# Low parts of weight units: a negated copy and an accumulating DMA in place of a subtraction

## The chip, the cores and the metric

The kernel runs on one core of one Trainium2 chip. Its time is that of one execution on the device, in microseconds; lower is better. A core has five engines that work side by side and wait for each other through semaphores: TensorE (matmuls), VectorE, ScalarE, GpSimd and SyncE, which here only starts transfers. Transfers between the chip's main memory and the core's on-chip memory are run by DMA engines; whichever engine starts one has it in its own queue and goes on.

## The reference

Two layers over 512 tokens of 1024 features, all in float32. Layer 0 mixes the tokens with a Mamba-2 state space (SSD), layer 1 with HGRN2. Behind the mixer of each layer comes a norm, a squared-ReLU MLP with 4096 hidden features, a second norm, and a gate with embeddings `p`:

```python
for i in range(DEPTH):
    mix = ssd_mixer(x, ...) if i % 2 == 0 else hgrn2_mixer(x, ...)
    h = layer_norm(DEEPNORM_ALPHA * x + mix, ln_g[i, 0], ln_b[i, 0])
    h = layer_norm(DEEPNORM_ALPHA * h + sq_relu_mlp(h, mlp_w1[i], mlp_w2[i]), ln_g[i, 1], ln_b[i, 1])
    x = h + jax.nn.sigmoid(h @ ple_w_gate[i]) * (p[i] @ ple_w_proj[i])
```

Nearly all of the arithmetic is matrix products with weights: the mixers' projections in and out (`u @ w_in`, `y @ w_out`), the MLP's `h @ w1` and `(a * a) @ w2`, and the gate's two.

## The kernel before

**Units.** A weight matrix comes in units of 128 partitions by 1024 float32 values, 512 KB. A matrix product in float32 is made as three products in the faster type float32r: both factors are split into a high part (the value rounded to float32r) and a low part (what is left of it), and `mm3` (line 109) makes high x high, high x low and low x high. So each unit needs, before TensorE can use it, a high and a low part. `unit` (line 98) does that for 192 plain units: SyncE loads the unit into a `raw` buffer (line 102), ScalarE casts it into `whi` (line 104), and VectorE subtracts `whi` from `raw` into `wlo` (line 106). `weight_sums` (line 284) does it for another 52 units of the MLP, two at a time, with sums of blocks for Strassen's product; its own casts and subtractions stand at lines 293 and 295.

**Buffers.** There are 3 `raw` buffers (`RAWS`), 5 of `whi` and 5 of `wlo`, used in turn by `unit` and `weight_sums` alike. A load waits until the `raw` buffer's earlier unit has been read by the cast and the subtraction; a cast waits until TensorE has done its last matmul with the earlier unit in that `whi`; TensorE waits for the cast before the first matmul with a high part, and for the subtraction before the first with a low part.

**Stages.** The SSD layer comes first (some 370 us): projections of 24 matmuls a unit (`project`, line 127), between them the scan's steps of each pair of heads, and the output projection. Then the MLP of layer 0: each eighth of the hidden features is projected (`hidden`, line 349), the first three pairs of tiles with plain units and the others with Strassen's products (`strassen`, line 309), and each eighth is projected out (`out_project`, line 225) with four plain units. The order is that of line 32: hidden eighth 0, then 1, then output 0, hidden 2, output 1 and so on; output 7 comes last and the second norm's chunks are made behind each of its four chunks of 128 tokens. An output projection adds, for each half of the columns and each of the four token chunks, twelve matmuls into one PSUM bank: six with the half's first unit, six with its second (`out_part`, line 208). The gate (lines 394 to 430) has, for each half of the columns, one unit of `wp` and four of `wg`, all five held over the four token chunks: six matmuls with the one into `pp`, twenty-four with the others into `pg`. Layer 1 has HGRN in the place of SSD, with the same MLP and gate behind it.

**What sets the order.** The kernel is written on a framework that plans the order of each engine's instructions ahead of time, by priorities and by its own estimates of how long each instruction takes; an engine then executes its own in that order, and waits at the head of it. What stands in `tc.high_priority(offset=LEAD)` (line 100) is planned earlier than its place in the code. Only in HGRN is the order of TensorE's instructions that of the code (`manual_schedule`, line 904), where the projections of later heads fill the waits of a head's scores. TensorE has four PSUM banks for projections (`psj`), so at most four chunks can be open at once.

The kernel's start is written with two units ahead of the others (lines 139 to 150): `first.append(unit(..., 0))`.

Of the kernel before, what the change touches and what calls it, by code (L numbers as in the profile page):

```python
# [27 lines left out]
RAWS = 3  # L28
FIRST = 1000
# the first pairs of hidden tiles are plain products, the others Strassen's  # L30
PLAIN = 3
ORDER = [(w[0], int(w[1])) for w in "h0 b0 h1 o0 h2 o1 h3 o2 h4 o3 h5 o4 h6 o5 h7 o6 o7".split()]
# HGRN: the projections in their order, and how much of them goes between the steps of two heads
# [9 lines left out]
def trunk(ctx: ExitStack, tc, a):  # L43
# [31 lines left out]
    def begin(name):  # L75
        """the pool of temporaries of a phase, in place of the phase before's"""
        if phase:
            phase[1].__exit__(None, None, None)
            phase.clear()
        phase.append(tc.tile_pool(name=name, bufs=1, reuse_waits="tile"))  # L80
        phase.append(phase[0].__enter__())
        phase.reverse()
        phase.append(bufs[name])
# [13 lines left out]
    # ---------------------------------------------------------------- weights  # L97
    def unit(src, lead=LEAD):
        n = src.shape[1]
        with tc.high_priority(offset=lead):  # L100
            raw = mk(raws, [P, 1024], "raw")
            nc.sync.dma_start(raw[:, :n], src)
            hi = mk(whip, [P, 1024], "whi", F32R)
            nc.scalar.copy(hi[:, :n], raw[:, :n])  # L104
            lo = mk(wlop, [P, 1024], "wlo", F32R)
            nc.vector.tensor_sub(lo[:, :n], raw[:, :n], f32(hi[:, :n]))  # L106
        return hi, lo
# [6 lines left out]
    class Split:  # L114
        """[128, n, 512] as high and low parts, in slots of four rows each."""
# [11 lines left out]
    def project(src, xs, ps, m=P, tok=slice(0, T)):  # L127
        """ps[m, tok] = W[:, tile].T @ x.T for a weight unit of eight row tiles."""
        hi, lo = src
        for k in range(8):  # L130
            c = slice(k * m, (k + 1) * m)
            mm3(ps[:m, tok], hi[:, c], lo[:, c], xs.h(k, tok), xs.l(k, tok), k == 0, k == 7)

    # ---------------------------------------------------------------- constants
# [5 lines left out]
    with tc.high_priority(offset=FIRST):  # L140
        for k0, n in ((0, 1), (1, 1), (2, 2), (4, 2), (6, 2)):
            nc.sync.dma_start(xraw[:, k0 : k0 + n, :], a["xT"][:, k0 : k0 + n, :])
            if k0 == 0:
                dtw = mk(raws, [P, 1024], "raw")
                nc.sync.dma_start(dtw[:, :256], a["wdt"])
            elif k0 in (1, 6):
                first.append(unit(a["wssd"][k0 // 4], 0))
            for k in range(k0, k0 + n):
                nc.scalar.copy(x_s.h(k), xraw[:, k, :])
                nc.vector.tensor_sub(x_s.l(k), xraw[:, k, :], f32(x_s.h(k)))  # L150
# [19 lines left out]
    # ---------------------------------------------------------------- layer norm and friends  # L170
# [7 lines left out]
    def layer_norm(c, gb):  # L178
        """acc[:, c] = LN(acc[:, c])"""
        src = acc[:, c, :]  # L180
        st = mk(sm, [P, 2, 6], "lnst")
        for h in range(2):
            nc.vector.bn_stats(st[:, h, :], src[:, h * 512 : (h + 1) * 512])
        mv = mk(sm, [P, 2], "lnmv")
        nc.vector.bn_aggr(mv, st.rearrange("p a b -> p (a b)"))
        sd = mk(sm, [P, 1], "lnsd")
        nc.scalar.activation(sd, mv[:, 1:2], AF.Sqrt, bias=eps)
        rs = mk(sm, [P, 1], "lnrs")
        nc.vector.reciprocal(rs, sd)
        nc.vector.scalar_tensor_tensor(src, src, mv[:, 0:1], gb[0], ALU.subtract, ALU.mult)  # L190
        nc.vector.scalar_tensor_tensor(src, src, rs, gb[1], ALU.mult, ALU.add)

    def transpose_split(src, dst, c, keep=None):
        """dst[:, k, chunk c] = src[tokens, k-th 128 features].T, split; unsplit in keep"""
        sl = slice(c * P, (c + 1) * P)
        for q in range(2):
            pt = bank(pst, "pt")
            for j in range(4):
                k = 4 * q + j
                nc.tensor.transpose(pt[:, j * P : (j + 1) * P], src[:, k * P : (k + 1) * P], ident)  # L200
            v = pt.rearrange("p (j t) -> p j t", j=4)
            h = dst.hi[q][:, :, sl]
            nc.scalar.copy(h, v)
            nc.vector.tensor_sub(dst.lo[q][:, :, sl], v, f32(h))
            if keep is not None:
                nc.scalar.copy(keep[q][:, :, sl], v)

    def out_part(units, n, xs, c, h, first, scale):
        """acc[:, c, half h] += x[:, chunk c].T @ W over n row tiles, each token's row by scale if given;
        acc holds alpha * residual (or the residual, if first)"""  # L210
        sl = slice(c * P, (c + 1) * P)
        ps = bank(psj, "pj")
        for k in range(n):
            hi, lo = units[k // 2]
            ks = slice((k % 2) * 512, (k % 2 + 1) * 512)
            mm3(ps, xs.h(k, sl), xs.l(k, sl), hi[:, ks], lo[:, ks], k == 0, k == n - 1)
        d = acc[:, c, h * 512 : (h + 1) * 512]
        if scale is not None:
            nc.vector.scalar_tensor_tensor(d, ps, scale[:, c : c + 1], d, ALU.mult, ALU.add)
        elif first:  # L220
            nc.vector.scalar_tensor_tensor(d, d, ALPHA, ps, ALU.mult, ALU.add)
        else:
            nc.vector.tensor_add(d, ps, d)  # L223

    def out_project(w, xs, first, after=None, scale=None):
        """w: the four units of four row tiles, by halves of the columns; after(c): what follows the last of chunk c"""
# [12 lines left out]
    def norm(i):  # L239
        """the norm's result, transposed and split, and what makes its chunk c"""  # L240
        gb = ln_params(i)
        h_s = Split(8)
        keep = [mk(b8, [P, 4, T], "b8") for _ in range(2)] if i % 2 == 0 else None

        def chunk(c):
            layer_norm(c, gb)
            transpose_split(acc[:, c, :], h_s, c, keep)

        return h_s, chunk, keep

    # Winograd's form of Strassen's product: seven products of blocks for eight. The blocks of h.T are
    # [token half][k half], those of the weights [k half][output tile].
    def block_sums(h_s, ht):
        """the four plain and four summed blocks of h.T, as (high, low) of a row tile k"""
# [28 lines left out]
    def weight_sums(src1, src2):  # L283
        """the seven blocks of two weight units: B11, B21, B22, T1, T2, T3, B21 - T2, as (high, low, column)"""
# [24 lines left out]
    def strassen(blocks, src1, src2, z):  # L309
        """z[:, m] = W[:, tile m].T @ h.T for two weight units"""  # L310
# [34 lines left out]
    def mlp_and_gate(layer, h_s, ht, last):  # L345
        """acc holds the normed h. Returns the next x, transposed and split, with x in acc."""
# [40 lines left out]
        # gate  # L387
# [45 lines left out]
    # ---------------------------------------------------------------- layer 0: SSD  # L433
    # time steps
# [36 lines left out]
    # dt * exp(cs_last - cs)  # L471
# [6 lines left out]
    def dt_tail():  # L478
        # token-major copies: [128 tokens, chunk, head]
# [10 lines left out]
    def conv_silu(ps, i, out):  # L490
        """out = silu(causal conv of ps + bias), channel tile i of the convolved ones"""
# [50 lines left out]
    def core(j, xs, sz, y, toks, btok, cbm, cm):  # L542
# [3 lines left out]
        # token-major x * dt and x * dt * decay to the chunk's end  # L546
# [11 lines left out]
        # chunk states and their scan  # L558
# [13 lines left out]
        # masked decays times C B  # L572
# [9 lines left out]
        # decay from the chunk's start, on channels  # L582
# [33 lines left out]
    def rms_group(ss):  # L616
        """1 / rms of each token of the group: [128 tokens, chunk]"""
# [52 lines left out]
    # ---------------------------------------------------------------- layer 1: HGRN2  # L670
# [6 lines left out]
    # lower bounds: softmax over the one layer, cumulated, less its first row  # L677
# [11 lines left out]
    # The tensor engine's order is fixed here: the projections of the heads to come fill the waits of a head's scores.  # L689
    def vg(i):  # L690
        """values and output gates of heads 2i and 2i + 1, by tokens: [128, chunk, 256]"""
# [80 lines left out]
    def hcore(h, s, i, hl):  # L772
# [12 lines left out]
        def column_sums(f, n):  # L785
            """the sums over the partitions, on each of them"""
# [8 lines left out]
        # the scores of a token with itself and of an odd one with the token before it  # L795
# [63 lines left out]
        # states  # L859
# [23 lines left out]
        # norm and output gate  # L883
# [57 lines left out]
def _tiles_m(w):  # L941
    """[K, M] -> [M/128, 128, K/128 * 128]: one unit per 128 output channels"""
# [4 lines left out]
def _tiles_g(w):  # L947
    """[K, 1024] -> [K/128, 128, 1024]: per four row tiles, two units for each half of the columns"""
# [5 lines left out]
def _tiles_h(w):  # L954
    """[K, 1024] -> [2 * K/256, 128, 2 * 512]: by halves of the columns, two row tiles each"""
# [5 lines left out]
def _tiles_q(w):  # L961
    """[1024, 1024] -> [4, 2, 128, 4 * 256]: by quarters of the columns, four row tiles each"""
# [4 lines left out]
def _cols(v):  # L967
    """[n * 128] -> [128, n]"""
# [3 lines left out]
def _rows(v):  # L972
    """[K, T] -> [128, K/128, T]"""
# [70 lines left out]
```

## Time and profile before

| | |
|---|---|
| median of 3 runs | 1495.58 us (1493.39 to 1496.82) |
| the profiled execution: span from the first to the last instruction | 1492.3 us |
| TensorE busy | 1479.3 us (99%) |
| VectorE busy | 1096.4 us (73%) |
| ScalarE busy | 711.2 us (48%) |
| GpSimd busy | 0.9 us |
| DMA engines, mean busy share by the loads' queue | 30.1%, 148.67 MB |
| granted TensorE clock | 0.999 |

The page has no time of the profiled execution other than its span; the median of the runs is 3.3 us above it.

How to read the rows: PE is TensorE's matmuls, PEld its loads of stationary operands, DVE VectorE, ACT ScalarE, POOL GpSimd, SPq the queue that SyncE starts transfers from. `wlo<-raw,whi` names what an instruction writes and reads, without buffer numbers; `x192` counts instructions; behind the bar stand the busy time in us, the mean of one in ns, and the idle time of the engine ahead of them with what ended most of it. In a timeline a row begins with its start and its duration in us, and `[0.53 <-DVE wlo L106]` says that the engine was idle for 0.53 us until VectorE's line 106 released it. The durations of matmuls overlap: they follow each other faster than one lasts. L-numbers are lines of the kernel before.

### The profile page before, as it was taken

The page shows a single profiled execution, that of the slowest core. Times are in us where ns is not written, and L with a number is a line of the kernel's source. Part 1 is how long each engine was busy: PE and PEld are TensorE (multiplying, and loading weights), DVE is VectorE, ACT ScalarE, POOL GpSimd, SP SyncE. Part 2 cuts the span into 40 slices and gives each one's busy share as a digit, 9 for nine tenths or more (in the row PEclk, how much of TensorE's full clock was granted, in tenths as well). Part 3 has the DMA queues.
Part 4 walks back from the last instruction along what each step waited for, and adds up shares of the span by engine and source line. Part 5 has one row for each costly group of instructions (what it writes and reads, how often), then busy time and mean ns, then how long its engine had stood idle before and what let it go on. Part 6 is the DMA issues. An engine that isn't in the chain of part 4 may idle for free.

```text
span 1492.3 us, 21964 instructions
## 1 busy us (share of the span) xinstructions
PE 1479.3 (99%) x8848; PEld 1280.9 (86%) x8848; DVE 1096.4 (73%) x1786; ACT 711.2 (48%) x968; POOL 0.9 (0%) x8
## 2 busy tenths in 40 slices
PE   8999999999999999999999999999999999999998
PEld 5888888888989999888778998989898999998887
DVE  6998677797886777776844767769787777777673
ACT  5777455563564434444334453543364444444342
POOL 0000000000000000000000000000000000000000
PEclk9999999999999999999999999999999999999999
DMA  6433223332233323244223222222123333324322
GB/s 237 169 102 111 98 100 113 100 113 85 71 99 99 113 82 103 88 139 129 94 71 114 86 66 77 70 72 72 57 72 99 114 113 100 110 79 150 115 71 71
DMA packets 41621, 150.07 MB, mean 101 GB/s; under 512 B 4624, under 2 KB 5136, under 8 KB 41392
## 3 DMA queue, kind: packets, MB, share of 16 engines
q1 hardware_dynamic: 41520, 148.67, 30.1%
q8 instruction: 70, 1.15, 0.3%
q14 instruction: 31, 0.25, 0.1%
HBM read 146.49 MB, written 2.16 MB: 100 GB/s over the span
## 4 chain that ended last, share of the span: by engine, by line
PE 97%; DMA 1%; DVE 1%; ACT 1%; issue 0%; SPq 0%; ACTq 0%; DVEq 0%
PE pj L110 29%; PE pj L111 28%; PE pj L112 28%; PE py L782 1%; PE py L591 1%; PE pt L200 1%; PE pm L561 1%; PE py L596 1%; PE py L792 1%; PE py L827 1%; DMA raw<-in_wg 1%; DVE wlo L106 0%; PE pt L549 0%; PE py L880 0%; PE py L112 0%; PE py L110 0%
## 5 line engine op out<-in xcount | busy, mean ns | idle before, releaser
L110 PE MATMUL pj<-whi,b 128*128 128x512 f32 (+1 forms) x1096 | 401.5, 367 | 0.5 <-ACT z L414 0.5
L111 PE MATMUL pj<-wlo,b 128*128 128x512 f32 (+1 forms) x1096 | 399.3, 364 | 0.5 <-DVE wlo L106 0.5
L112 PE MATMUL pj<-whi,b 128*128 128x512 f32 (+1 forms) x1096 | 399.8, 365 | 0.0
L110 PE MATMUL pj<-b,whi 128*128 128x256 f32 (+1 forms) x1024 | 348.0, 340 | 2.1 <-ACT whi L104 2.1
L112 PE MATMUL pj<-b,wlo 128*128 128x256 f32 (+1 forms) x1024 | 344.2, 336 | 0.0
L111 PE MATMUL pj<-b,whi 128*128 128x256 f32 (+1 forms) x1024 | 343.7, 336 | 0.0
L104 ACT CAST whi<-raw 128x1024 fp32r<-128x1024 f32 x192 | 201.4, 1050 | 229.6 <-PE pj L111 133.4
L106 DVE TENSOR_TENSOR wlo<-raw,whi 128x1024 fp32r<-128x1024 f32 x192 | 233.9, 1220 | 64.4 <-ACT whi L104 62.4
L111 PEld LDWEIGHTS pj<-wlo,b 128*128 128x128 f32 x1096 | 206.8, 189 | 32.2 <-DVE wlo L106 1.0
L110 PEld LDWEIGHTS pj<-whi,b 128*128 128x128 f32 x1096 | 206.6, 189 | 32.3 <-ACT z L414 0.7
L112 PEld LDWEIGHTS pj<-whi,b 128*128 128x128 f32 x1096 | 206.7, 189 | 31.7 <-issue 0.2
L110 PEld LDWEIGHTS pj<-b,whi 128*128 128x128 f32 x1024 | 194.5, 190 | 22.0 <-ACT whi L104 4.7
L112 PEld LDWEIGHTS pj<-b,wlo 128*128 128x128 f32 x1024 | 194.4, 190 | 20.3 <-DVE b L150 1.7
L111 PEld LDWEIGHTS pj<-b,whi 128*128 128x128 f32 x1024 | 194.6, 190 | 18.3 <-issue 1.9
L293 ACT CAST whi<-raw 128x1024 fp32r<-128x1024 f32 (+1 forms) x52 | 43.4, 835 | 136.2 <-PE pj L112 110.4
L223 DVE TENSOR_TENSOR acc<-pj,acc 128x512 f32<-128x512 f32 x120 | 81.6, 686 | 35.0 <-PE pj L112 34.5
L110 PE MATMUL pj<-S,whi 128*128 128x256 f32 x312 | 87.4, 280 | 0.0
L111 PE MATMUL pj<-S,whi 128*128 128x256 f32 x312 | 87.0, 279 | 0.0
L112 PE MATMUL pj<-S,wlo 128*128 128x256 f32 x312 | 87.0, 279 | 0.0
L295 DVE TENSOR_TENSOR wlo<-raw,whi 128x1024 fp32r<-128x1024 f32 (+1 forms) x52 | 49.7, 957 | 35.0 <-ACT whi L293 35.0
L293 ACT CAST whi<-a 128x1024 fp32r<-128x1024 f32 x26 | 27.3, 1050 | 94.8 <-PE pj L111 45.5
L110 PEld LDWEIGHTS pj<-S,whi 128*128 128x128 f32 x312 | 58.7, 188 | 0.0
(217 smaller groups left out, 1810.6 us busy)
## 6 DMA issues: line engine op xcount, KB each, us to landing
raw<-in_w SPq DMA_DIRECT2D x128, 512.0 KB, 3.4
raw<-in_wssd SPq DMA_DIRECT2D x40, 512.0 KB, 3.4
a<-csd SPq DMA_DIRECT2D x16, 512.0 KB, 4.0
raw<-in_wso SPq DMA_DIRECT2D x16, 512.0 KB, 3.3
raw<-in_wg SPq DMA_DIRECT2D x16, 512.0 KB, 3.8
raw<-in_whvg SPq DMA_DIRECT2D x16, 512.0 KB, 3.3
raw<-in_whq SPq DMA_DIRECT2D x16, 512.0 KB, 3.3
raw<-in_who SPq DMA_DIRECT2D x8, 512.0 KB, 3.3
```

The source lines that it names most:

```text
L104: nc.scalar.copy(hi[:, :n], raw[:, :n])
L106: nc.vector.tensor_sub(lo[:, :n], raw[:, :n], f32(hi[:, :n]))
L110: nc.tensor.matmul(out, sh, mh, start=start, stop=False)
L111: nc.tensor.matmul(out, sh, ml, start=False, stop=False)
L112: nc.tensor.matmul(out, sl, mh, start=False, stop=stop)
L200: nc.tensor.transpose(pt[:, j * P : (j + 1) * P], src[:, k * P : (k + 1) * P], ident)
L223: nc.vector.tensor_add(d, ps, d)
L293: nc.scalar.copy(hi[:, :n], f)
L295: nc.vector.tensor_sub(lo[:, :n], f, f32(hi[:, :n]))
L561: nc.tensor.matmul(pst_[:, c * P : (c + 1) * P], btok[:, c, :], xw[:, c].rearrange("p h q -> p (h q)"), start=True, stop=True)
L591: nc.tensor.matmul(yd[64 * r : 64 * r + 64, sl], xdt[:, 2 * c + r, :], m[:, r, sl], start=True, stop=True)
L596: nc.tensor.matmul(yo[:, c * P : (c + 1) * P], pv[:, c - 1].rearrange("p h q -> p (h q)"), cm[:, c * P : (c + 1) * P], start=True, stop=True,)
```

## The change

In `unit`, all but the first two units (`early=True`) get their low part in another way. ScalarE, having cast `raw` into `whi`, also writes the negative of `whi` into `wlo`. Then a transfer started from GpSimd's queue reads `raw` and adds it to what stands in `wlo`, so that `wlo` holds `raw - whi`. The `raw` buffer is read by that transfer in place of the subtraction, and there are four of them in place of three. The units that `weight_sums` makes for Strassen's products are as before. (The diff also empties the lines of comments; that is left out here.)

```diff
-RAWS = 3
+RAWS = 4
...
-    def unit(src, lead=LEAD):
+    def unit(src, lead=LEAD, early=False):
         n = src.shape[1]
         with tc.high_priority(offset=lead):
             raw = mk(raws, [P, 1024], "raw")
             nc.sync.dma_start(raw[:, :n], src)
             hi = mk(whip, [P, 1024], "whi", F32R)
             nc.scalar.copy(hi[:, :n], raw[:, :n])
             lo = mk(wlop, [P, 1024], "wlo", F32R)
-            nc.vector.tensor_sub(lo[:, :n], raw[:, :n], f32(hi[:, :n]))
+            if early:
+                nc.vector.tensor_sub(lo[:, :n], raw[:, :n], f32(hi[:, :n]))
+            else:
+                nc.scalar.mul(lo[:, :n], f32(hi[:, :n]), -1.0)
+                nc.gpsimd.dma_start(lo[:, :n], raw[:, :n], accum_op=ALU.add)
         return hi, lo
...
-                first.append(unit(a["wssd"][k0 // 4], 0))
+                first.append(unit(a["wssd"][k0 // 4], 0, True))
```

## The prediction

> **What bounds the kernel now.** I read the page first (busy time, groups, DMA issues), then the windows by stage, then who waits for the line that goes, then the timeline at the few places where a weight unit is made just in time.
>
> From the page (engine: busy us, share, instructions; a group's busy us and mean ns; an issue's KB and median us to landing):
>
> ```profile
> span 1492.3 us, 21964 instructions
> PE 1479.3 (99%) x8848; PEld 1280.9 (86%) x8848; DVE 1096.4 (73%) x1786; ACT 711.2 (48%) x968; POOL 0.9 (0%) x8
> ...
> q1 hardware_dynamic: 41520, 148.67, 30.1%
> ...
> L104 ACT CAST whi<-raw 128x1024 fp32r<-128x1024 f32 x192 | 201.4, 1050 | 229.6 <-PE pj L111 133.4
> L106 DVE TENSOR_TENSOR wlo<-raw,whi 128x1024 fp32r<-128x1024 f32 x192 | 233.9, 1220 | 64.4 <-ACT whi L104 62.4
> ...
> raw<-in_w SPq DMA_DIRECT2D x128, 512.0 KB, 3.4
> ...
> a<-csd SPq DMA_DIRECT2D x16, 512.0 KB, 4.0
> ```
>
> TensorE is idle for 1492.3 - 1479.3 = 13.0 us of the span, so nothing that only relieves VectorE can win more. The windows (PE busy of each stretch in its second figure) say where these 13.0 us lie:
>
> ```profile
> 0.00:25.00 25.00, 18.74 (x62) 9.46 (x63) 13.28 (x20) 12.50 (x19) 0.88 (x8) 1.00 0.73 263
> ...
> 415.00:710.00 295.00, 295.00 (x1821) 266.53 (x1820) 213.48 (x300) 130.94 (x142) 0.00 (x0) 1.00 0.34 109
> 710.00:795.00 85.00, 84.22 (x407) 68.16 (x406) 57.20 (x76) 33.09 (x45) 0.00 (x0) 1.00 0.26 86
> 795.00:1065.00 270.00, 268.61 (x1879) 239.17 (x1877) 187.41 (x389) 123.37 (x248) 0.00 (x0) 1.00 0.23 75
> ...
> 1405.00:1492.30 87.30, 82.76 (x401) 68.71 (x399) 52.13 (x71) 26.79 (x36) 0.00 (x0) 0.99 0.22 73
> ```
>
> 6.3 us are the start, 4.5 us the last stretch with its tail, 0.8 and 1.4 us the first gate and HGRN. And of line 106, who waited for it in the whole run:
>
> ```profile
> L106 DVE TENSOR_TENSOR wlo<-raw,whi x192: 1197/1220/1253, 9.2 to 1463.4; 128x1024 fp32r<-128x1024 f32 x192
> ...
>   PEld pj L111: 1.0, 1
>   PE pj L111: 0.5, 1
>   PEld pj L112: 0.4, 1
> ```
>
> TensorE lost 1.9 us to the subtraction that the change removes. That is what there is to win; what there is to lose is decided by how long the replacement takes between "high part made" and "low part there", against the time that TensorE leaves.
>
> **The change part by part.**
>
> *Removed:* 190 of the 192 subtractions, 190 x 1.220 = 232 us of VectorE, 73% to 58%. VectorE isn't the bound and nearly nobody waits for it: worth 0 to 1.9 us.
>
> *Added on ScalarE:* 190 negated copies of 128x1024. The nearest row is an ACTIVATE of that shape (timeline: start us, us):
>
> ```profile
> 508.43 1.06 ACT L370 ACTIVATE z<-z 128x1024 f32<-128x1024 f32 x1
> ```
>
> 190 x 1.06 = 201 us, 48% to 61%. In sum it lies beside the matmuls; where casts follow each other closely it makes each unit take 2.1 us of ScalarE instead of 1.05, which counts below.
>
> *Added on GpSimd's queue and the DMA engines:* 190 transfers of 512 KB that read raw, read lo and write lo. GpSimd is idle (0.9 us busy), and its queue holds nothing else after the start, so waiting there holds up nobody. In bytes, 190 x 0.524 = 99.6 MB; read twice it is 199 MB against the 148.67 MB that take 30.1%, so 40% more: 70% in the mean. Not the bound, but loads and these transfers will meet.
>
> *The time D from issue to landing* of such a transfer isn't in this trace. Below: a load of the same 512 KB, 3.4 us. Above: the largest transfer there is,
>
> ```profile
> acc<-in_x SPq DMA_DIRECT2D x1, 2048.0 KB, 8.7
> ```
>
> 8.7 us for four times the bytes. From the two rows (8.7 - 3.4) / 3 = 1.8 us for each 512 KB and 1.6 us fixed; two streams instead of one give 1.6 + 2 x 1.8 = 5.2 us. I take 5.4 us, with 0.2 us for landing beside the loads (the csd row, landing among them, is 4.0 and not 3.4), and keep 3.4 and 8.7 for the range. The Trainium skill, DMA: Bandwidth & Descriptors, section Anatomy of one DMA — SWDGE (gpsimd) path, gives a fixed 2.0 us plus bytes / 436e3, an estimate of 3.2 us here for one pass; no run here shows a transfer from that queue.
>
> *Moved, the wait.* The low part is now ready D + 1.06 us after the cast ends, before it was 1.2 us. So at every unit I compare that with the time from the cast's end to TensorE's first use of the low part. Where the casts run several units ahead of TensorE, in the SSD stage and most of HGRN, I cost it at nothing; that lead hides it. The lead is gone where the five slots of whi and wlo are all in use and a cast waits for TensorE to free one. ScalarE's and TensorE's rows there:
>
> ```profile
> 507.48 1.05 ACT L104 CAST whi<-raw 128x1024 fp32r<-128x1024 f32 x1 [0.82 <-PE pj L111]
> ...
> 513.16 1.05 ACT L104 CAST whi<-raw 128x1024 fp32r<-128x1024 f32 x1 [1.38 <-PE pj L111]
> ```
> ```profile
> 517.64 0.40 PE L111 MATMUL pj<-wlo,b 128*128 128x512 f32 x1
> ...
> 519.02 0.39 PE L111 MATMUL pj<-wlo,b 128*128 128x512 f32 x1
> ```
>
> *(a) An output projection behind Strassen's products.* Its first unit's cast ends at 508.53 and its low part is read at 517.64: 9.1 us, enough for any D up to 8. The second's cast waits for TensorE to free a slot, ends at 514.21 and is read at 519.02: 4.8 us. Too late by D + 1.06 - 4.8 = D - 3.7, with 5.4: 1.7 us. The order of the hidden tiles has seven such places in each layer: 14 x 1.7 = 24 us if TensorE's order stays. But while it waits the other three token chunks have their first unit's matmuls ready (six of some 0.23 us each), so 4.1 us of work could be pulled ahead.
>
> *(b) The start of the gate,* where all five slots turn over, and its second half:
>
> ```profile
> 725.89 1.05 ACT L104 CAST whi<-raw 128x1024 fp32r<-128x1024 f32 x1 [0.34 <-PE pj L112]
> ...
> 730.49 0.39 PE L111 MATMUL pj<-wlo,b 128*128 128x512 f32 x1
> ...
> 736.05 0.50 PE L111 MATMUL pj<-wlo,b 128*128 128x512 f32 x1 [0.53 <-DVE wlo L106]
> ...
> 742.56 0.39 PE L110 MATMUL py<-whi,a 128*128 128x512 f32 x1
> ```
> ```profile
> 758.07 1.05 ACT L104 CAST whi<-raw 128x1024 fp32r<-128x1024 f32 x1
> 759.46 1.05 ACT L104 CAST whi<-raw 128x1024 fp32r<-128x1024 f32 x1 [0.34 <-PE pj L112]
> 761.67 1.05 ACT L104 CAST whi<-raw 128x1024 fp32r<-128x1024 f32 x1 [1.15 <-DMA raw<-in_wg]
> ...
> 763.54 0.39 PE L111 MATMUL pj<-wlo,b 128*128 128x512 f32 x1
> ```
>
> At the start 730.49 - 726.94 = 3.55 us, too late by D - 2.5 = 2.9 us; in the second half 763.54 - 759.12 = 4.4 us, too late by D - 3.4 = 2.0 us. Both in two layers: 9.8 us. The units behind them follow at 1.4 us (758.07 to 759.46, six matmuls), and ScalarE now needs 2.1 us for each: 0.7 us lost for each of seven units in two layers, 9.8 us in a fixed order; other chunks can cover half, 4.9 us.
>
> *(c) The start of HGRN,* whose matmul order is written by hand, and the fourth unit of the last output projection of each layer:
>
> ```profile
> 786.15 1.05 ACT L104 CAST whi<-raw 128x1024 fp32r<-128x1024 f32 x1 [0.81 <-PE py L112]
> ...
> 792.10 0.28 PE L111 MATMUL pj<-wlo,b 128*128 128x256 f32 x1
> ```
>
> 792.10 - 787.20 = 4.9 us, too late by 1.6 us, and some 0.7 us more for the second unit through ScalarE: 2.3 us. The fourth unit's cast and first use,
>
> ```profile
> 705.20 1.05 ACT L104 CAST whi<-raw 128x1024 fp32r<-128x1024 f32 x1 [8.46 <-PE pj L112]
> ...
> 710.67 0.39 PE L111 MATMUL pj<-wlo,b 128*128 128x512 f32 x1
> ```
>
> are 4.4 us apart: 2.0 us too late, 4 us in both layers, with other chunks to draw on as in (a).
>
> *RAWS 3 to 4, and SP's queue.* SP's waits:
>
> ```profile
> SPq L102 <- DVE wlo L106: 577.8, 123, 21.7
> ```
>
> SP waits at 123 loads for the subtraction that frees a raw buffer; now it waits for the transfer's landing, 1.06 + 5.4 - 1.2 = 5.3 us longer. Behind the waiting load stand the next loads in order, those of Strassen's units and csd too, and ScalarE's casts wait for them. A fourth buffer gives a third more time, so I cost the loads at nothing: at (a) the casts wait for TensorE and not for raw, as their releasers say. If that cover went, each late load would cost its lateness at the same places. At the gate it takes away the wait for raw that the 736.05 row shows the end of: 0.5 us there, with its like in the other layer about 1 to 2 us won. The two units of the start keep the subtraction, so the 6.3 us of the start stay.
>
> *The sum.* Everything in a fixed order: 24 + 9.8 + 9.8 + 2.3 + 4 = 50 us. What other chunks can't cover: 9.8 + 4.9 + 2.3 = 17 us, less 2 us for raw: 15 us. Between them stands the planner, which orders TensorE's matmuls outside HGRN. The 742.56 row shows that it does depart from the code: pp's matmul stands first in a chunk and came 12 us after pg's. But it goes by its own idea of D. I take a quarter of (a) and of the fourth units as uncovered, 7 us, and get 22 us. The profiled span becomes 1514; the median of the runs is 3.3 us over the span shown, so 1517.5.
>
> **The rivals.**
>
> *Fixed order, or a long D.* The planner thinks the transfer short and leaves the order, so TensorE stands still at all places: 1495.6 + 50 - 2 = 1544. With D at 8.7 us, 3.3 us more at each of the 22 places (14 + 4 + 2 + 2), 1544 + 73 = 1617. For it: 14 places of one pattern and no slack in TensorE. Against: the chunks that are ready.
>
> *Covered: no change.* With D at 3.4 us (a) and the second half of the gate are on time, and only 0.9 us at two gate starts is left, against 1 to 2 us won: 1496. For it: loads of this size take 3.4 us. By the skill's page named above, 3.2 us, it would come out here. Against: two streams are read and not one.
>
> *Faster.* The low parts are on time everywhere and the fourth raw buffer removes the gates' waits: 1.9 us for line 106 and the 0.8 + 1.4 us of idle at the gate and HGRN, with the second gate's like, 4 to 5 us: 1491. It decides where D + 1.06 is under 3.55, so D under 2.5 us, or where the planner covers the gate's starts too. Against: no 512 KB transfer here lands that fast.
>
> *The DMA engines fill up.* 33 units in 415 to 710 add 33 x 2 x 0.524 = 34.6 MB, at 331 GB/s (148.67 MB in 30.1% of 1492.3 us) 104 us in 295, from a share of 0.34 to 0.69. Not full; if the adding runs at half that rate it is, the loads come late, and it is the long D above.
>
> **How the numbers follow.** Forecast, partly covered, 1517 (1501 to 1540): 0.52. Fixed order or long D, with full engines: 0.21. Covered: 0.15. Faster: 0.12. About 0.2%, 3 us, is what a measurement of this kernel can tell from no change. So faster 0.12, same 0.15, slower 0.73. The range reaches from 1493, into the faster case, to 1560, which leaves out some of the fixed order and the long D: about 0.2 in all.
>
> **What the profile after would show.** VectorE near 865 us and ScalarE near 910; 190 transfers of 512 KB from GpSimd's queue with their time to landing, my D; TensorE's idle time up from 13 to some 35 us, with waits for wlo from a DMA at lines 111 and 112; in the windows 415 to 710 and 1120 to 1405 no longer full. If these waits are few and D over 5 us, the planner covered them. I am wrong if D is under 3 us, or if the order of the matmuls changes so much that the places above no longer exist.

## The result and the profile after

| | before | after |
|---|---|---|
| median of four runs each, us | 1494.49 (1492.72 to 1496.82) | 1606.63 (1602.02 to 1611.14) |
| profiled span, us | 1492.3 | 1602.6 |
| TensorE not busy in the span, us | 13.0 | 92.7 |
| granted TensorE clock | 0.999 | 0.985 |

The ratio is 1.0748, with an interval of 1.0735 to 1.0761: the change makes the kernel 112 us slower. The forecast was 1517, with a range up to 1560; the time lies outside it. The sign was right, the size wrong by a factor of five (22 us forecast, 112 measured).

The page after, the rows that answer those of before (busy time and groups, queues with packets, MB and share of the 16 engines, the chain, DMA issues with KB and median us to landing):

```profile
span 1602.6 us, 22563 instructions
PE 1509.9 (94%) x8848; PEld 1293.1 (81%) x8848; DVE 889.3 (55%) x1596; ACT 873.5 (55%) x1150; POOL 164.7 (10%) x198
...
q0 software_dynamic: 27360, 99.63, 33.9%
q1 hardware_dynamic: 41520, 148.67, 27.0%
...
PE 55%; issue 19%; DMA 16%; DVE 5%; ACT 4%; SPq 0%; POOL 0%; POOLq 0%; DVEq 0%; ACTq 0%
...
L115 PE MATMUL pj<-wlo,b 128*128 128x512 f32 (+1 forms) x1096 | 411.0, 375 | 68.3 <-DMA wlo<-raw 68.3
...
L110 POOL DMA_DIRECT2D wlo<-raw x190 | 163.9, 865 | 1407.3 <-ACT wlo L109 1346.2
...
L109 ACT ACTIVATE wlo<-whi 128x1024 fp32r<-128x1024 f32 x190 | 198.4, 1054 | 2.0
...
wlo<-raw POOLq DMA_DIRECT2D x190, 512.0 KB, 5.7
```

VectorE has lost 207 us of work, and ScalarE has gained 162. None of that shows in the time. What shows is the 68.3 us behind the bar of line 115: TensorE standing at the first matmul with a low part until the transfer has landed. The span grew by 110 us; 80 of them are idle TensorE (13.0 to 92.7) and 31 are TensorE busy for longer with the same 8848 matmuls.

Who waited for whom (engine, line, releaser: us in total, times, longest); first three rows of the kernel after, then one of the kernel before:

```profile
PE pj L115 <- DMA wlo<-raw: 68.3, 33, 3.6
SPq L102 <- DMA wlo<-raw: 851.6, 133, 25.3
DVE a L304 <- DMA raw<-in_w: 42.3, 12, 5.4
```
```profile
DVE a L300 <- DMA raw<-in_w: 5.1, 9, 1.8
```

With those of line 116 (6.2 us) and of the gates' `py` (2.0 us) these are 38 waits, 76.5 us of the growth of 80, and not hundreds. Five of them, 7.5 us in sum, lie where the prediction put nothing (one early in the SSD stage, the others at the mixers' output projections and the MLPs' first units); the others sit at the few places that it listed. The last two rows show a side effect: the first of Strassen's sums on VectorE waited 5.1 us for its loads before, and waits 42.3 us now, because a `raw` buffer comes free later.

The windows after by stage (stretch, its length, then busy us of PE, PEld, DVE, ACT and POOL with instructions, granted clock, DMA share, GB/s):

```profile
0.00:25.00 25.00, 18.94 (x61) 9.40 (x62) 11.22 (x18) 14.20 (x20) 2.74 (x10) 1.00 0.80 263
411.00:769.00 358.00, 337.64 (x2036) 300.62 (x2036) 203.69 (x304) 176.70 (x199) 30.12 (x35) 0.99 0.56 146
769.00:833.00 64.00, 48.91 (x202) 37.15 (x201) 19.21 (x28) 23.72 (x31) 6.88 (x8) 0.92 0.63 153
833.00:1130.00 297.00, 293.26 (x2005) 259.75 (x2003) 156.29 (x364) 170.63 (x300) 35.32 (x41) 1.00 0.60 144
1130.00:1556.00 426.00, 398.65 (x2332) 350.84 (x2333) 240.90 (x358) 203.96 (x240) 36.18 (x42) 0.97 0.56 145
1556.00:1602.60 46.60, 35.79 (x174) 28.98 (x173) 8.61 (x14) 13.54 (x17) 4.30 (x5) 0.97 0.43 102
```

The MLP of layer 0, which had no idle time at all before, has 20.4 us (358.00 - 337.64), and the gate of layer 0 15.1 us in 64. The MLP and the first half of the gate of layer 1 lose 27.4 us, the last stretch 10.8. Set against the times of the same events before, the growth by stage, beside what the prediction put there:

| stage | measured, us | forecast, us |
|---|---|---|
| SSD | +10 | 0 |
| MLP, layers 0 and 1 | +27.5, +30.5 | 7 in sum |
| gates of both layers, with the start of HGRN | +23, +18 | 17, less 2 for raw |
| rest of HGRN | +1 | 0 |
| sum | +110 | 22 |

**One of the fourteen places.** The second unit of an output projection behind Strassen's products, in the kernel after. ScalarE (cast and negated copy), GpSimd (the issue), TensorE (the last matmul ahead of the wait, and the first behind it); each row starts with its start and its duration:

```profile
531.69 1.05 ACT L104 CAST whi<-raw 128x1024 fp32r<-128x1024 f32 x1 [0.58 <-PE pj L115]
532.77 1.06 ACT L109 ACTIVATE wlo<-whi 128x1024 fp32r<-128x1024 f32 x1
```
```profile
534.12 0.86 POOL L110 DMA_DIRECT2D wlo<-raw  x1 [4.01 <-ACT wlo L109]
```
```profile
537.32 0.39 PE L114 MATMUL pj<-whi,b 128*128 128x512 f32 x1
541.31 0.50 PE L115 MATMUL pj<-wlo,b 128*128 128x512 f32 x1 [3.60 <-DMA wlo<-raw]
```

This is the sum of the prediction's step (a), row by row: the cast ends at 532.74, the copy at 533.83, GpSimd has the issue at 534.12, and TensorE is let go at 541.31, 7.2 us later. TensorE came to the matmul 4.97 us after the cast (537.71; 4.8 was forecast). It stands for 3.60 us. And it stands at once after the six matmuls of the first chunk's first unit: the order is the old one, with no matmul of another chunk in between.

**The slow matmuls behind the wait.** Windows around that place and around another (columns as above):

```profile
538.00:541.50 3.50, 0.19 (x1) 0.19 (x2) 0.00 (x0) 3.47 (x4) 0.78 (x1) 1.00 1.04 200
541.50:545.00 3.50, 3.50 (x10) 2.72 (x10) 1.58 (x2) 0.04 (x1) 0.00 (x0) 0.55 1.06 180
545.00:548.00 3.00, 3.00 (x14) 2.48 (x13) 0.53 (x2) 0.00 (x0) 0.00 (x0) 0.96 0.94 339
```
```profile
1289.50:1292.90 3.40, 1.22 (x6) 0.67 (x4) 0.07 (x1) 3.40 (x5) 1.72 (x2) 0.98 1.08 214
1292.90:1296.30 3.40, 3.35 (x8) 2.68 (x9) 0.81 (x2) 1.62 (x2) 0.00 (x0) 0.52 1.09 202
1296.30:1299.00 2.70, 2.70 (x14) 2.22 (x13) 1.01 (x1) 0.00 (x0) 0.00 (x0) 1.00 0.96 217
```

Behind the wait the clock falls to about a half for some 3.4 us (0.55 and 0.52 in windows that don't quite meet its edges), ten matmuls are done where there would be fifteen or sixteen, and then it is whole again. The trace after has eleven such stretches between the start and the end, nine of 3.4 us and two of twice that, 44 us in sum, the trace before none. TensorE was busy in 42 of the 44 us, so at half speed they account for 21 of the 31 us that it was busy longer. The Trainium skill, TensorE: Matmul & The Clock Gate, section Part 1: The HAM clock gate, has a free-running window of 4096 cycles, 3413 ns, and a clock that is either half or whole; the lengths here agree with it. Its section HAM oscillation — how this bites in real kernels puts the limit at idle gaps over some 3.4 us; here an idle time of 2.2 us (the second place) was followed by half clock too, while others of 2.0 to 3.2 us were not.

Which ones, the trace tells. Its records of the clock put the starts of all eleven stretches on one grid of 3.413 us. In each cell of this grid that ran at whole clock one can add up TensorE's idle time: where it was 1.94 us or more, half clock followed in the next cell, and where it was 1.83 us or less, it didn't. Two cells around the wait of 3.20 us that ends at 35.04, and the two at the first of the two places above (columns as there):

```profile
29.84:33.25 3.41, 2.00 (x9) 1.31 (x7) 3.41 (x6) 3.24 (x5) 0.26 (x1) 1.00 1.01 269
33.25:36.66 3.41, 1.62 (x7) 1.36 (x8) 3.41 (x6) 1.33 (x3) 0.00 (x0) 1.00 1.08 238
538.42:541.83 3.41, 0.52 (x2) 0.48 (x3) 0.00 (x0) 3.08 (x4) 0.35 (x1) 1.00 1.03 198
541.83:545.25 3.42, 3.42 (x9) 2.65 (x9) 1.82 (x2) 0.00 (x0) 0.00 (x0) 0.50 1.05 189
```

The wait of 3.20 us is cut by a border into 1.4 and 1.8 us, and the clock stays whole; the wait of 3.60 us leaves 2.9 us in one cell, and the next runs at 0.50. So whether a wait of 2 to 3.6 us costs clock depends on where the border falls. In the traces of all the runs a limit of 1.85 us parts the 83 whole-clock cells that were followed by half clock from the other 6071, but for six.

The same windows show the DMA share at 1.04 to 1.09 while TensorE waits: the DMA engines, 61% busy in the mean (33.9 + 27.0), are full at these places (a share of 1.00 to 1.10 in the 3.5 us before each of the fourteen waits, 0.45 and 0.34 in 411 to 446 and 460 to 492; a share of one and a little more means that they always had a packet).

**The gate.** The first gate after, TensorE's five waits and GpSimd's issues there (the last row but one of GpSimd's stands for two):

```profile
810.71 0.50 PE L115 MATMUL py<-wlo,a 128*128 128x512 f32 x1 [0.79 <-DMA wlo<-raw]
815.14 0.50 PE L115 MATMUL pj<-wlo,b 128*128 128x512 f32 x1 [2.07 <-DMA wlo<-raw]
818.88 0.50 PE L115 MATMUL pj<-wlo,b 128*128 128x512 f32 x1 [1.65 <-DMA wlo<-raw]
822.39 0.50 PE L115 MATMUL pj<-wlo,b 128*128 128x512 f32 x1 [1.63 <-DMA wlo<-raw]
828.08 0.50 PE L115 MATMUL pj<-wlo,b 128*128 128x512 f32 x1 [3.13 <-DMA wlo<-raw]
```
```profile
809.43 0.86 POOL L110 DMA_DIRECT2D wlo<-raw  x1 [2.46 <-ACT wlo L109]
811.32 1.81 POOL L110 DMA_DIRECT2D wlo<-raw  x2 [1.03 <-ACT wlo L109]
818.84 0.86 POOL L110 DMA_DIRECT2D wlo<-raw  x1 [5.71 <-ACT wlo L109]
```

Three transfers issued within 2.8 us (809.43 to 812.2) land 3.7 and 3.5 us apart (815.14, 818.88, 822.39): they share the DMA engines, and each takes its own 3 us of all sixteen (33.9% of 1602.6 us over 190 transfers is 2.9 us). TensorE eats a unit in 1.4 us.

**The start.** In the SSD stage, where the prediction costed the change at nothing, TensorE stands early on:

```profile
24.14 0.91 POOL L110 DMA_DIRECT2D wlo<-raw  x1 [5.74 <-ACT wlo L109]
27.20 0.86 POOL L110 DMA_DIRECT2D wlo<-raw  x1 [2.15 <-ACT wlo L109]
```
```profile
35.04 0.50 PE L116 MATMUL pj<-b,wlo 128*128 128x512 f32 x1 [3.20 <-DMA wlo<-raw]
```

The transfer issued at 24.14 lands at 35.0, 10.9 us later, beside the first loads; the two behind it take 10.8 and 12.1. The first window above had a share of 0.80. This wait is 3.2 of the stage's 10 us. Two more for low parts, at SSD's output projection (0.6 at 378 us) and at the MLP's first unit (1.3 at 410 us), make it 5.0; another 4.1 us are waits for VectorE's steps of the scan at 71 and 93 us, which the kernel before doesn't have and whose cause wasn't traced.

### The profile page after: what moved, and what is told of

It is laid out like the page before. It is cut to its first block, busy times and chain, and to the rows that moved or that the text cites. A ratio compares the mean times of both kernels' runs of the same rounds, so it can differ in the third digit from the quotient of the medians.

```text
span 1602.6 us, 22563 instructions
## 1 busy us (share of the span) xinstructions
PE 1509.9 (94%) x8848; PEld 1293.1 (81%) x8848; DVE 889.3 (55%) x1596; ACT 873.5 (55%) x1150; POOL 164.7 (10%) x198
## 3 DMA queue, kind: packets, MB, share of 16 engines
q0 software_dynamic: 27360, 99.63, 33.9%
## 4 chain that ended last, share of the span: by engine, by line
PE 55%; issue 19%; DMA 16%; DVE 5%; ACT 4%; SPq 0%; POOL 0%; POOLq 0%; DVEq 0%; ACTq 0%
PE pj L115 16%; PE pj L116 15%; PE pj L114 15%; DMA wlo<-raw 9%; DMA raw<-in_w 4%; DMA raw<-in_wssd 1%; PE py L786 1%; DVE wlo L299 1%; DMA a<-csd 1%; PE py L595 1%; ACT wlo L109 1%; ACT whi L104 1%; DVE b L307 1%; PE py L600 1%; PE pm L565 1%
## 5 line engine op out<-in xcount | busy, mean ns | idle before, releaser
L115 PE MATMUL pj<-wlo,b 128*128 128x512 f32 (+1 forms) x1096 | 411.0, 375 | 68.3 <-DMA wlo<-raw 68.3
L114 PE MATMUL pj<-whi,b 128*128 128x512 f32 (+1 forms) x1096 | 406.9, 373 | 0.6 <-ACT z L418 0.5
L116 PE MATMUL pj<-whi,b 128*128 128x512 f32 (+1 forms) x1096 | 406.8, 371 | 0.0
L110 POOL DMA_DIRECT2D wlo<-raw x190 | 163.9, 865 | 1407.3 <-ACT wlo L109 1346.2
L115 PEld LDWEIGHTS pj<-wlo,b 128*128 128x128 f32 x1096 | 211.1, 193 | 112.9 <-DMA wlo<-raw 81.2
L114 PEld LDWEIGHTS pj<-whi,b 128*128 128x128 f32 x1096 | 210.9, 192 | 35.3 <-ACT z L418 0.7
L116 PEld LDWEIGHTS pj<-whi,b 128*128 128x128 f32 x1096 | 211.3, 193 | 32.1
L109 ACT ACTIVATE wlo<-whi 128x1024 fp32r<-128x1024 f32 x190 | 198.4, 1054 | 2.0
L500 DVE SCALAR_TENSOR_TENSOR cv<-pj,cst,cv 128x509 f32<-128x509 f32 (+2 forms) x72 | 53.3, 745 | 33.6 <-ACT cv L497 32.3
```

The source lines that it names most:

```text
L109: nc.scalar.mul(lo[:, :n], f32(hi[:, :n]), -1.0)
L110: nc.gpsimd.dma_start(lo[:, :n], raw[:, :n], accum_op=ALU.add)
L114: nc.tensor.matmul(out, sh, mh, start=start, stop=False)
L115: nc.tensor.matmul(out, sh, ml, start=False, stop=False)
L116: nc.tensor.matmul(out, sl, mh, start=False, stop=stop)
L500: nc.vector.scalar_tensor_tensor(cv[:, d:], ps[:, : T - d], convw[:, i, k : k + 1], cv[:, d:], ALU.mult, ALU.add)
```

## The experiments

Theory W, in the expectations, is that TensorE's time goes where the low part comes too late, at the listed places, and nowhere else. Each experiment is a change of the kernel after, unless it says otherwise; ratios are against the kernel before, on the same chip.

**What ScalarE and the buffers cost.** The kernel before with four `raw` buffers:

```diff
-RAWS = 3
+RAWS = 4
```

> The kernel before with four raw buffers in place of three, nothing else. Theory W (the loss comes from units whose low part lands after TensorE wants it, at few places with little lead, and from the half clock behind the long ones): 1491 to 1496 us, at most the gates' waits for raw are won. Rival P (the planner's other order, set off by the fourth buffer and the other prices, costs the time): over 1500.

Measured: 1493.14 us, 0.9983 (0.9974 to 0.9992). The fourth buffer alone wins 2.6 us, slightly more than the 1 to 2 us of the prediction. And the change with VectorE in the place of the DMA: ScalarE still makes all the negated copies.

```diff
-                nc.gpsimd.dma_start(lo[:, :n], raw[:, :n], accum_op=ALU.add)
+                nc.vector.tensor_add(lo[:, :n], raw[:, :n], f32(lo[:, :n]))
```

> The negated copy on ScalarE stays, and VectorE adds raw to it in place of the transfer, with four raw buffers. So ScalarE's 190 copies are there without the DMA. W: 1492 to 1500, the low part is 1.1 us later than before, and the shortest lead behind a cast is 3.5 us. If ScalarE's copies were the cost: 1520 or more.

Measured: 1493.43 us, 0.9991 (0.9981 to 1.0000). Its page:

```profile
PE 1480.5 (99%) x8848; PEld 1281.1 (86%) x8848; DVE 1101.8 (74%) x1786; ACT 874.8 (59%) x1152; POOL 0.9 (0%) x8
```

ScalarE does as much as in the kernel after (874.8 us against 873.5), and TensorE loses nothing. So none of the 112 us are ScalarE's; all come with the transfer.

**Where the loss lies.** The change in SSD and HGRN alone (92 units), then in the MLPs and gates alone (98 units); the others keep the subtraction:

```diff
+    mlp = [False]
...
-            if early:
+            if early or mlp[0]:
```
```diff
-            if early:
+            if early or not mlp[0]:
```

> The change in the SSD and HGRN layers alone (92 of the 190 units); the units of the MLP and the gate keep VectorE's subtraction. W: 1500 to 1508, since nearly all of these units have 10 to 30 us of lead; what is left is the SSD layer's 10 us. Rival R (each transfer costs time through the DMA engines and ScalarE wherever it is): half of 112, 1550.

> The converse: the change in the MLP and the gate alone (98 of the 190 units). W: 1585 to 1600. R: 1550. Both parts' differences should add up to about 112 if the places are independent.

Measured: 1509.24 us, 1.0099 (1.0082 to 1.0116), and 1580.84 us, 1.0581 (1.0560 to 1.0601). Nearly the same number of units costs 13.5 us in the one (slightly over the expected 1508) and 85 us in the other (slightly under the expected 1585). Its place decides what a transfer costs, not how many there are. The two don't add up to the whole as expected: 99 of 112 us, so some 13 us come only where both parts have the change, and no run tells where. In the kernel with the loose units alone TensorE waits 4.3 us for a low part at 30 us, 2.4 us at the start of HGRN and 1.8 us at two other places, and 3.3 us at 90 us for a step of VectorE's in the scan; elsewhere, where the casts run ahead, it waits for nothing new.

The gates' 20 units back to the subtraction:

```diff
-            pu = unit(a[f"wp_{layer}"][h])
-            gu = [unit(a[f"wg_{layer}"][4 * h + j]) for j in range(4)]
+            pu = unit(a[f"wp_{layer}"][h], early=True)
+            gu = [unit(a[f"wg_{layer}"][4 * h + j], early=True) for j in range(4)]
```

> The changed kernel with VectorE's subtraction kept for the 20 units of the two gates. The gates took some 38 us of the 112, for the transfers of five units in a row land 3 to 3.6 us apart and TensorE uses one up in 1.4 us: 1567 to 1575. If ScalarE's second pass made the gates late: 1585 or more.

Measured: 1578.29 us, 1.0572 (1.0539 to 1.0606): 28 us less than the whole change, a little short of what was expected. The gates' waits are gone from the trace.

**Why the transfer is slow.** The transfer copies `raw` in place of adding it, so this kernel leaves out the subtraction of the high part, and only its time is of use:

```diff
-                nc.gpsimd.dma_start(lo[:, :n], raw[:, :n], accum_op=ALU.add)
+                nc.gpsimd.dma_start(lo[:, :n], raw[:, :n])
```

> The changed kernel with the transfer copying raw over lo in place of adding to it, so its low parts are wrong by the high parts (the rest is as it was). Theory S (a transfer that adds reads two streams, which makes its 5.7 us and, in bursts, some 3 us from one landing to the next): landing near 4 us, the queue's share from 33.9% to some 18%, the time 1550 or less. Rival G (GpSimd's issue of 0.86 us and the landing make D, whatever is read): landing over 5 us and 1595 to 1607.

Measured, in two runs: 1525.62 us, 1.0202 (1.0181 to 1.0222). Its queue and its issues:

```profile
q0 software_dynamic: 27360, 99.63, 18.9%
...
wlo<-raw POOLq DMA_DIRECT2D x190, 512.0 KB, 3.3
```

The same 99.63 MB from the same queue land in 3.3 us instead of 5.7, and take 18.9% of 1523.0 us, 288 us of sixteen engines, where adding took 33.9% of 1602.6, 543 us: 1.9 times as much. Nearly three quarters of the loss (81 of 112 us) hang on the adding, not on GpSimd's queue. The Trainium skill, Collectives: The Full Stack, section The bandwidth ceiling: the fold count and why AG ≠ RS ≠ AR, says of a reduce-scatter between cores that it is slower than an all-gather, which only copies, not by the sum itself but by the two reads that the sum needs, with a measured ratio of 1.93. The 1.9 here is close to it, though no run here tells the second read from the sum itself.

**Whether the order could have covered it.** Two attempts to give TensorE something in the wait at the fourteen places: twelve useless matmuls between the first chunk's two units, and then the real cover, all four chunks' first units ahead of any second unit, by hand.

```diff
+            if k == 2 and dummies:
+                pm = bank(psm, "pm")
+                for _ in range(dummies):
+                    nc.tensor.matmul(pm, xs.h(0, sl), units[0][0][:, :512], start=True, stop=True)
```
```diff
+                if scale is None and h == 0:
+                    ps = [bank(psj, "pj") for _ in range(NCH)]
+                    for u in range(2):
+                        for c in range(NCH):
...
+                                mm3(ps[c], xs.h(k, sl), xs.l(k, sl), units[u][0][:, ks], units[u][1][:, ks], k == 0, k == 3)
```

> The changed kernel with 12 matmuls without use (2.7 us of work, results unread) between the first and the second unit's matmuls in the first chunk of the 14 output projections behind Strassen's products. They take the place of idle time and add no other. If the half clock comes from TensorE's idle time, its dips in the MLP go and the time falls by 6 to 14 us, to 1592 to 1600. If it has another cause, 1607 or more.

> The changed kernel with these 14 output projections' first halves in another order: the first unit's matmuls of all four token chunks, then the second unit's. That is the cover which the prediction took the planner to find. If it was there to be had, the waits at the second unit go with their half clock: 1607 less 45 to 55, 1552 to 1562. If the banks or the scan of evictions forbid it: above 1590.

Both missed in the time: 1619.01 us, 1.0821 (1.0794 to 1.0847), and 1631.23 us, 1.0916 (1.0893 to 1.0940), both slower than the change itself. The waits for `wlo` at the covered places were nearly all gone, and with the useless matmuls so was the half clock behind them, as expected; but a new wait had come, for a PSUM bank: 12 waits, 16.2 us in sum, with the useless matmuls, and 12 of some 4 to 5.7 us, 54.0 us in sum, with the covered chunks. The kernel with the covered chunks, VectorE and then TensorE behind one of the places:

```profile
449.12 1.23 DVE L314 TENSOR_TENSOR wlo<-raw,whi 128x1024 fp32r<-128x1024 f32 x1 [2.99 <-ACT whi L312]
457.76 0.69 DVE L319 TENSOR_TENSOR a<-raw,raw 128x512 f32<-128x512 f32 x1 [7.42 <-DMA raw<-in_w]
458.37 0.69 DVE L322 TENSOR_TENSOR b<-raw 128x512 f32<-128x512 f32 x1
458.98 1.22 DVE L393 TENSOR_TENSOR b<-z,b 128x1024 fp32r<-128x1024 f32 x1
460.11 0.68 DVE L320 TENSOR_TENSOR a<-raw,a 128x512 f32<-128x512 f32 x1
460.71 0.68 DVE L251 SCALAR_TENSOR_TENSOR acc<-acc,pj 128x512 f32<-128x512 f32 x1
```
```profile
461.54 0.77 PE L114 MATMUL pj<-whi,b 128*128 128x512 f32 x1 [4.96 <-DVE acc L251]
```

And ahead of it GpSimd's issue of an accumulating transfer and SyncE's of the load that the sum at 457.76 waits for:

```profile
443.70 0.87 POOL L110 DMA_DIRECT2D wlo<-raw  x1 [3.88 <-ACT wlo L109]
```
```profile
449.90 0.33 SPq L308 DMA_DIRECT2D raw<-in_w  x1
```

Read backwards: TensorE waits 4.96 us for a PSUM bank that VectorE's line 251 (an eviction) empties. The eviction stands in VectorE's queue behind a sum of Strassen's next units, and that sum waits 7.42 us for its load. The load is late because its `raw` buffer was held until the transfer issued at 443.70 had landed: by the trace at 449.84, and the load was issued at 449.90. Beside the next transfers it then took 7.8 us itself. So the cover was real, and the prediction's other free item, the loads, took it back.

That reading was tested: the same order with a fifth `raw` buffer, and, beside it, the fifth buffer without the order. Room for it comes from two tiles of HGRN and four very small ones.

```diff
-RAWS = 4
+RAWS = 5
...
-    bufs = dict(..., hgrn=dict(two, xs=4, sz=4, cv=4, ...
+    bufs = dict(..., hgrn=dict(two, xs=4, sz=3, cv=3, ...
```

> The kernel of the first units for all four chunks (1631 us, waits of 4 to 5.7 us of TensorE for an eviction of VectorE at 12 places), with five raw buffers in place of four; to make room, two scratch tiles of HGRN have three buffers in place of four and four tiles of under 40 bytes have one, so only the MLP layers are compared. Theory H (a transfer that adds holds its raw buffer until it lands; the next Strassen load is issued late; VectorE, whose queue is in order, stands at the sum that reads it, and the evictions stand behind it): with a fifth buffer the wait of VectorE's sum for its load falls from 82 us to under 30, the 12 waits of 4 to 5.7 us fall under 1.5 each, and the part from 411 us to the first gate is 30 us or more shorter in layer 0. Rival B (four banks taken at once, the eviction itself): waits and time stay within 10 us of 1631.

> The change with five raw buffers in place of four and the same room made for them, the order of the chunks untouched. Theory H (at the fourteen places the time from issue to landing decides, the raw buffers only where VectorE's evictions stand behind a late load): waits at the second units stay at 2 to 3.6 us, the time stays within 12 us of 1607. Rival: the late loads already cost the change itself much of its 58 us in the MLP layers, then 1560 to 1585.

Measured: 1545.80 us, 1.0335 (1.0306 to 1.0364), and 1606.86 us, 1.0739 (1.0723 to 1.0755). The MLP of layer 0, from the same point to the wait for the gate's first unit, of the one and of the other:

```profile
411.00:745.00 334.00, 331.77 (x2052) 297.29 (x2051) 206.22 (x306) 178.48 (x202) 30.11 (x35) 1.00 0.59 160
```
```profile
411.00:780.00 369.00, 344.22 (x2030) 304.54 (x2028) 206.88 (x306) 177.96 (x200) 30.12 (x35) 0.95 0.52 142
```

With order and buffer TensorE idles 2.2 us in this stretch, with the buffer alone 24.8. The eviction waits of 4 to 5.7 us were gone, as theory H had it (one wait of 0.9 us, for another line of VectorE, is left in the whole run); the stretch is 41 us shorter than with the order and four buffers (375 us). In one point the expectation missed: VectorE's sum still waits 62.6 us for its loads in all, not under 30,

```profile
DVE a L319 <- DMA raw<-in_w: 62.6, 23, 5.1
```

but in 23 waits of at most 5.1 us instead of 12 of up to 7.6, and the evictions now reach the banks in time. A fifth buffer alone wins nothing (1606.86 against 1606.63; its waits at the seven places of layer 0 are 2.6 to 4.1 us, a little over the expected 2 to 3.6), and the order alone loses; together they win 61 us.

**The places, once more from the other side.** Only the second units at the fourteen places back to the subtraction, and then the gates' units as well:

```diff
-                units = [unit(w[2 * h + i]) for i in range(2)]
+                units = [unit(w[2 * h + i], early=scale is None and h == 0 and i == 1) for i in range(2)]
```

> The change, except that at the fourteen places the second of the two units of the first half is made by VectorE's subtraction again (14 of 190 units); first units, gates, SSD and HGRN keep the accumulating transfer. Theory P (the place decides: at these units TensorE waits 2 to 3.6 us for the transfer each time, 38 us in all, and nine windows of half clock stand behind those waits): the two MLP layers lose nearly all of the 58 us that they gained, and the time falls to 1545 to 1560. Rival Q (the sum of the transfers on the engines and of the raw buffers' holding decides, wherever they are): 14 of 190 transfers less is 7% of 112 us, 1595 to 1602.

> As the run before it in this set, and the gates' 20 units by subtraction too, so that 156 of 190 units keep the accumulating transfer. Theory P: what is left is SSD's and HGRN's part (13.5 us where only they had the change) and a few us at the first units, so 1508 to 1525. Rival Q (the sum of transfers): 156 of 190 leaves 82% of 112 us, 1580 to 1590.

Measured: 1550.45 us, 1.0347 (1.0323 to 1.0372), and 1520.38 us, 1.0159 (1.0144 to 1.0174). Theory P held in both. 14 of 190 transfers carried 56 of the 112 us; the gates' 20 another 30; the other 156 the remaining 26 us. In the first of the two no half clock is left in the MLPs up to the last output projections, so the slow stretches there do belong to these waits.

## Why the prediction was wrong, point by point

- **What bounds the kernel, VectorE's relief, ScalarE's copies: right.** 207 us less on VectorE are seen nowhere in the time, and 190 copies at a forecast 1.06 us (measured 1.054) cost nothing, shown by the kernel in which VectorE does the adding: 0.9991. (Instruction by instruction VectorE lost 232 us and ScalarE's copies took 200, as forecast; records of neighbours overlap, so the busy times moved by less.) Of the 1.9 us to be won only 0.5 were waits of matmuls, the others were waits of loads of stationary operands; no step hangs on that.
- **D, 5.4 us: nearly right.** The median is 5.7 us (4.5 to 12.1). That the adding makes it so long is shown by the plain copy's 3.3 us; that it is the second stream, the reason given, fits but isn't shown apart. The margin of 0.2 us for landing beside the loads was too small: the figure for the program isn't the D of the places. At the second units in the MLP of layer 0 it was 5.6 to 7.1 us, 6.3 in the mean, with the DMA engines full around the waits, plus 0.3 us before the issue. The forecast said of the engines that 70% is not full. The mean was even lower, 61%; at the places the share was 1 and above.
- **The budgets at the places: right.** 4.8 us forecast, 4.97 measured; and the waits are D + 1.06 + 0.3 - 4.8 within a few tenths.
- **Step (a), "I take a quarter of (a) and of the fourth units as uncovered": the step that failed.** The planner left TensorE's order as it was, so none was covered. All fourteen waits stand in the trace, of 1.6 to 3.7 us. The rival "fixed order", at 0.21 with long D, named this. Waits of 38 us in the two MLPs (with half clock and the rest: 58 us) stood in the place of 7. That other chunks can cover it is shown by the order written by hand with a fifth buffer; that they would cover it was a hope about the planner, and the only evidence for it (one row with an order unlike the code) came from another stage.
- **Loads at nothing: wrong as a price, right only while the order stays.** A fifth buffer changes nothing in the kernel as it is. But once the waits at the places are covered, the late release of `raw` reaches TensorE through VectorE's queue and costs more than the cover wins (1631). "A fourth buffer gives a third more time" compared buffers with loads on average; a transfer holds its buffer longer (5.3 us in the forecast), and VectorE's wait for loads rose from 5.1 to 42.3 us.
- **Gate, step (b): right place, wrong queue.** I let the units follow each other at ScalarE's pace, 0.7 us lost for each; they follow at the transfers' pace, 3.5 us each against TensorE's 1.4. The gates with the start of HGRN cost 41 us in place of 15.
- **SSD at nothing: wrong, 10 us.** The lead of several units doesn't exist yet in the first 35 us, and there D is 11 to 12 us beside the first loads: 3.2 us. Another 1.8 us are two short waits for low parts near the stage's end; of the rest 4.1 us are waits for VectorE in the scan, whose cause stays open.
- **Not in the prediction at all: the clock.** About 21 us, a fifth of the loss, come from half clock behind the waits. Even the rival with everything in a fixed order (1544) was too low for that reason and for the two above; its higher end (1617 with D at 8.7) is near the result by the wrong D.
- **The fourth `raw` buffer: right.** 1 to 2 us forecast, 2.6 measured.

## What to carry over

A hand-off that moves from an engine beside the data to a DMA costs little where units are made well ahead, and all of its latency that exceeds the lead where they are made just in time: count the just-in-time places in the trace and price each with the latency under the traffic of that place, not with the mean. Treat cover by a planner as absent until the order shows it, and add, for each wait that can leave TensorE idle for some 1.9 us within one cell of 3.4 us, half of the next cell, 1.7 us. A transfer that reads a buffer also holds it until it lands, and the wait for that can come back through an engine whose queue is in order.

## What the runs showed of the hardware beyond expectation

- A 512 KB transfer within the on-chip memory that adds takes 2.9 us of all sixteen DMA engines and lands 5.7 us after its issue (median); the same one that copies takes 1.5 us and lands after 3.3 us. Its issue keeps GpSimd busy for 0.86 us.
- Transfers issued back to back from GpSimd's queue share the engines: three within 2.8 us landed 3.5 to 3.7 us apart.
- TensorE's clock is set for cells of 3.413 us on a fixed grid: behind a cell at whole clock with more than some 1.85 us of idle time in sum (1.94 and 1.83 are the nearest on either side in the kernel after) the next runs at half. A wait of 2.0 us in one cell was enough, and one of 3.2 us across a border was not. It stays at half for a second cell where the first held 0.6 us of idle time or more (the nearest cells of all runs: 0.62 stayed, 0.53 didn't).
- Of the 31 us that TensorE was busy longer, 21 are half clock; the other 10 weren't traced to a cause.
